# Eight residual stores issued from GpSimd's queue, and two PSUM banks shared in the odd mixer

## The chip, the cores and the metric

The kernel runs on one core of a Trainium2 chip. The metric is device microseconds (us) of one execution, the median of several runs. The engines are TensorE (PE in the rows; PEld is its weight load), VectorE (DVE), ScalarE (ACT), GpSimd (POOL) and SyncE (SP), which here only issues DMAs. Each engine works through its own instructions in order; an instruction that waits holds up all that stand behind it on its engine.

## The reference

One inference step of a two-layer trunk. The even layer (0) runs SSD heads and RG-LRU blocks, the odd layer (1) runs 4 GLA heads and 8 HGRN heads. Each layer is a mixer and a squared-ReLU MLP, each followed by a layer norm over the residual sum:

```python
for layer in range(DEPTH):
    if layer % 2 == 0:
        mixed, (a1, a2, a3, a4) = _even_mixer(h, segs, (ssd[j], ssd_conv[j], rg[j], rg_conv[j]), p, j)
        ...
    else:
        mixed, (a5, a6) = _odd_mixer(h, segs, (gla[j], hgrn[j]), p, j, layer)
        ...
    h = _layer_norm(ALPHA * h + mixed, p['ln1_g'][layer], p['ln1_b'][layer])
    h = _layer_norm(ALPHA * h + _sq_relu_mlp(h, p['mlp_w1'][layer], p['mlp_w2'][layer]),
                    p['ln2_g'][layer], p['ln2_b'][layer])
```

Both kinds of odd heads run the same gated linear attention, in chunks, over the prompt (16 meta and 512 prompt tokens) and over 8 samples of 8 tokens that start from given states:

```python
def step(s, inp):
    q_c, k_c, v_c, bl_c = inp
    o = jnp.einsum('bthk,bhkv->bthv', q_c, s)
    s = s * jnp.exp(bl_c)[..., None] + jnp.einsum('bshk,bshv->bhkv', k_c, v_c)
    return s, o
```

## The kernel before

Activations lie transposed in SBUF as 8 tiles of 128 features by T = 592 tokens (16 meta, 64 of the samples, 512 of the prompt), split into a high and a low float32r part (`h`). Every projection is a `Task`: two halves of the tokens, each 24 matmuls (L182) of 128x296 (some 128x280) into one of 5 PSUM banks (`pm`), after which ScalarE or VectorE reads the bank. Weights come as 512 KB units over SP's queue into 3 `raw` buffers (L120) and are split by ScalarE (L126) and VectorE (L127) a few units ahead.

Between the halves of tasks, `weave()` runs one step of each active generator, so that the small matmuls of the attention stand between the large ones on TensorE. These small products share the other 3 PSUM banks (`px`), which are handed out in turn; a fourth call of `px()` gets the first bank again, and its first matmul waits until that bank was read. Dependencies in PSUM are kept by whole banks. A scheduler then sets the final order on each engine, within what depends on what; the excerpts below show that order.

The places that the change touches:

- The end of layer 0's MLP (`after` in `mlp`). When the last half of the layer norm is done, GpSimd adds the norm's bias to each of the 8 residual tiles `rs[k]` (L645, 128x592), and each tile is stored to DRAM as `res` (L646, 296 KB), to be read back in layer 1's output projection (L511). SyncE issues the stores, between weight loads ahead of them and, behind them, the loads of the odd mixer: `wg2` (L1126, 64 KB, shown as `wg` in the rows), two masks, a head's states `sin` (L1159, 1 MB) and further weights.
- The start of the odd mixer. The tasks of the low-rank gate (L247, read into `lgf` by L1376) and of q, k and two v's of the first GLA head run half by half. Then `decays()` makes the decay `ls` of each of the 4 GLA heads from `wg2` and `lgf`: two matmuls (L1387, four rows in the trace), ScalarE (L1388) and VectorE (L1389, which writes `ls`). The tile `ls` of the second head lies where a residual tile lay, so its first writer waits for that tile's store; so do `q` of the first head and some others.
- `attend`, run for each head: nv = 2 value tiles for GLA, nv = 1 for HGRN. It transposes the prompt's values (L1195, two banks when nv = 2, copied to SBUF by L1196), the stacked sample values (L1218, one bank), and the samples' values (L1222, copied to `vs` by L1223); for nv = 2, L1222 has a bank of its own, of which it fills 256 of 512 columns. Later come transposes of the keys (L1243), scores (L1247, L1261, L1262), the samples' read of their states (L1270, 256 of 512 columns, copied by L1273), the samples' output (L1281, L1282: a bank of which 64 or 128 columns are used, copied by L1284) and the nine state products. For nv = 1 these are L1291 (four), L1295 (four) and L1298 (the ninth, a bank of its own); VectorE adds them into `sin` (`update`, L1287), and `sin` is stored (L1314). Then follow the prompt's states (L1321, VectorE L1322).

Of the kernel before, what the change touches and what calls it, by code (L numbers as in the profile page):

```python
# [14 lines left out]
P = 128  # L15
# [56 lines left out]
def _trunk(ctx, tc, nc, I, O):  # L72
    V, A, G, PE = nc.vector, nc.scalar, nc.gpsimd, nc.tensor
# [14 lines left out]
    def px():  # L88
        return pxp.tile([P, 512], F32, tag="px", name="px")
# [9 lines left out]
    def vc(name, i=0, n=1):  # L99
        o = VEC[name] + i  # L100
        return vec[:, o:o + n]

    def mk(name):
        a, b = MSK[name]
        return msk[:, a:b]

    ident, umask, lsmask, uxmask, lxmask, seqm, sel, blk = (
        mk(n) for n in ("ident", "u", "ls", "ux", "lx", "seq", "sel", "blk"))
# [205 lines left out]
    def new_h():  # L314
        return [act_tile(hp, "h") for _ in range(KT)]
# [231 lines left out]
    def mlp(H, layer, halves, last, keep=None):  # L547
# [3 lines left out]
        with ExitStack() as st:  # L551
# [3 lines left out]
            rs = [rp.tile([P, T], F32, tag="r", name="r") for _ in range(KT)]  # L555
# [83 lines left out]
            def after(i):  # L639
                if not last and out[0] is None:  # L640
                    out[0] = new_h()
                norm.finish(i, out[0])
                if keep is not None and i == 1:
                    for k in range(KT):
                        G.tensor_scalar(rs[k], rs[k], vc("ln2b", layer * 8 + k), None, OP.add)  # L645
                        nc.sync.dma_start(keep[:, k], rs[k])  # L646

            run([w1(0, f) for f in W1_ORDER[:4]], by_half=True)
            for k, f in enumerate(W1_ORDER[4:]):
# [3 lines left out]
            for b in range(4):  # L653
                if b < 3:
                    run([w1(b + 1, f) for f in W1_ORDER[:2]])
                    for j in range(0, KT, 2):
                        w2_pair(b, j)
                    run([w1(b + 1, f) for f in W1_ORDER[2:]])
                else:
                    run([w2(b, j) for j in range(KS)])  # L660
                    norm.shift()
                    run([w2(b, j) for j in range(KS, KT)], by_half=True, after=after)
# [458 lines left out]
    def odd_mixer(H, g):  # L1121
# [28 lines left out]
        def attend(q, k, ls, sc, qs, vf, gate, gcol, sdram, sout, pout, more):  # L1150
# [4 lines left out]
            nv = len(vf)  # L1155
            N = nv * P
# [33 lines left out]
            vs = sd.tile([P, 256], F32, tag="vs", name="vs")  # L1190
            for v in range(nv):
                p = px()
# [22 lines left out]
            p = px()  # L1215
            for v in range(nv):
                for j in range(2):
                    PE.transpose(p[0:120, j * N + v * P:j * N + (v + 1) * P],  # L1218
                                 vst[:, v, j].rearrange("p r c -> p (r c)").bitcast(F32), ident)
            u = px() if nv > 1 else p[:, 256:512]  # L1220
            for v in range(nv):
                PE.transpose(u[:, v * P:(v + 1) * P], vf[v][:, 16:144], ident)  # L1222
            A.copy(vs[:, 0:N], u[:, 0:N])  # L1223

            mw = sd.tile([P, 9, P], F32R, tag="mw", name="mw")
            mn = sd.tile([P, 2, 256], F32R, tag="mn", name="mn")
# [13 lines left out]
            p = px()  # L1240
# [5 lines left out]
            p = px()  # L1246
# [10 lines left out]
            p = px()  # L1257
# [6 lines left out]
                              cmask[:, None, 0:P].to_broadcast([P, 4, P]), p.rearrange("p (c n) -> p c n", n=P))  # L1264

            p = px()
            for j in range(2):
                for b in range(4):
                    w = 64 * b + 32 * j
                    PE.matmul(p[32 * b:32 * b + 32, 0:N], qm[:, w:w + 32], sin[:, 4 * j + b],  # L1270
                              start=(j == 0), stop=(j == 1), tile_position=(0, 32 * b))
# [7 lines left out]
            p = px()  # L1279
# [6 lines left out]
            def update(b, p, n):  # L1286
                V.tensor_tensor(sin[:, b:b + n], sin[:, b:b + n], p.rearrange("p (b n) -> p b n", b=n), OP.add)  # L1287

            if nv == 1:
                p = px()  # L1290
                PE.matmul(p, mn[0:120, 0, 0:P], mw[0:120, 0:4].rearrange("p b n -> p (b n)"), start=True, stop=True)  # L1291
                V.tensor_copy(S[:, 0, 0:P], p[:, 0:P])
                update(0, p[:, P:], 3)
                p = px()
                PE.matmul(p, mn[0:120, 1, 0:P], mw[0:120, 4:8].rearrange("p b n -> p (b n)"), start=True, stop=True)  # L1295
                update(3, p, 4)
                p = px()
                PE.matmul(p[:, 0:P], mn[0:120, 1, 0:P], mw[0:120, 8], start=True, stop=True)  # L1298
                update(7, p[:, 0:P], 1)
            else:  # L1300
                for b0 in range(0, 9, 2):
                    if b0 == 4:
                        yield
                    p = px()
                    n = min(2, 9 - b0)
                    for b in range(b0, b0 + n):
                        PE.matmul(p[:, (b - b0) * N:(b - b0 + 1) * N], mw[0:120, b], mn[0:120, 0 if b < 4 else 1],
                                  start=True, stop=True)
                    if b0 == 0:
                        V.tensor_copy(S[:, 0], p[:, 0:N])  # L1310
                        update(0, p[:, N:], 1)
                    else:
                        update(b0 - 1, p[:, 0:n * N], n)
# [3 lines left out]
            for c0 in range(0, 4, 4 // nv):  # L1317
                p = px()
# [7 lines left out]
            for v in range(nv):  # L1326
                p = px()
# [18 lines left out]
            rs = g("rs")  # L1346
            for c0, c1 in TAIL:
                p = px()[:, 0:c1 - c0]
# [46 lines left out]
        for h in range(4):  # L1395
            q, k, v0, v1 = (g(n) for n in ("q", "k", "v", "v"))
            tasks = [copy_task(q, TAIL), copy_task(k, FULL), copy_task(v0, FULL), copy_task(v1, FULL)]
            if h == 0:
                run([Task(H, FULL, lr_consume, small=wsr[:, 1])] + tasks[0:NB], by_half=True)
                run(tasks[NB:])  # L1400
            else:
                run(tasks)
            z = [g("zs"), g("zs")]
            while len(lsg) <= h:
                weave()
            active.append(attend(q, k, lsg[h], 1.0 / 16, P ** -0.5, (v0, v1), z, hg[:, 0:2],
                                 I["gst"][h], O["gla_s"][h], O["gla_p"][h], 1))
            run([silu_task(z[0]), silu_task(z[1])])
# [17 lines left out]
        for h in range(8):  # L1426
            if h == 0:
                run([f_task(0)])
            q, v, z = g("q"), g("v"), g("zs")
            run([silu_task(q), copy_task(v, FULL)])  # L1430
            ls, k = fk[h]
            active.append(attend(q, k, ls, 1.0, 0.5, (v,), (z,), hg[:, 2:3],
                                 I["hst"][h], O["hgrn_s"][h], O["hgrn_p"][h], 1 if h in (0, 7) else 0))
            run([silu_task(z)])
            if h < 7:
                run([f_task(h + 1)])
        return ys, st.close

    with ExitStack() as st:
        gp = pool("ge", NGE, stack=st)  # L1440

        def g(name="g"):
            return gp.tile([P, T], F32, tag="g", name=name)
# [174 lines left out]
```

## Time and profile before

| | |
|---|---|
| time before, median of 3 runs | 1945.5 us (1942.92 to 1948.19) |
| the profiled execution, its own time | 1947.84 us |
| its span in the trace | 1946.0 us |
| TensorE matmuls busy | 1869.0 us (96%) |
| VectorE / ScalarE / GpSimd busy | 1298.0 / 886.8 / 412.5 us |
| granted TensorE clock, mean | 0.98 |
| odd mixer's stretch of the span, about | 916 to 1460 us |

TensorE is busy nearly throughout, so that what matters are the stretches in which it is not. Times within the span count from its start. A clock of 1.00 is 2.4 GHz, 0.50 is 1.2 GHz.

### The profile page before, as it was taken

How to read it: one execution, taken by the hardware profiler on the slowest of the kernel's cores; microseconds unless marked ns; L12 is line 12 of the kernel's file. 1: busy time of each engine (PE TensorE's matmuls, PEld its weight loads, DVE VectorE, ACT ScalarE, POOL GpSimd, SP SyncE). 2: the span in 40 equal slices, each digit the busy share in tenths (PEclk: the TensorE clock that was granted, in tenths of full speed). 3: DMA queues.
4: the chain of work that ended last, by engine and by line, in shares of the span. 5: the costliest groups of instructions: out<-in, count | busy, mean ns of one | idle time of the engine just before them, and what ended most of it. 6: DMA issues, size and time to landing. Idle time of an engine off the chain costs nothing.

```text
span 1946.0 us, 33588 instructions
## 1 busy us (share of the span) xinstructions
PE 1869.0 (96%) x13854; PEld 1828.1 (94%) x13854; DVE 1298.0 (67%) x2035; ACT 886.8 (46%) x1550; POOL 412.5 (21%) x427
## 2 busy tenths in 40 slices
PE   8998899999999999999999999999999899999996
PEld 8998899898999999998899999999999899999996
DVE  7896767868875757458645456565665877676637
ACT  5333245623644444324544455665642563534333
POOL 3454423114000000135121222121203200000014
PEclk9999899999999999999999999999999899999998
DMA  6232221321223132312332223223232123141411
GB/s 203 90 118 72 68 100 55 121 88 55 77 66 109 66 109 66 114 61 93 109 111 102 99 96 106 89 86 104 90 114 66 66 66 123 52 130 44 130 55 49
DMA packets 69273, 175.97 MB, mean 90 GB/s; under 512 B 6624, under 2 KB 30304, under 8 KB 67968
## 3 DMA queue, kind: packets, MB, share of 16 engines
q1 hardware_dynamic: 69120, 173.82, 26.6%
q8 instruction: 109, 1.79, 0.4%
q14 instruction: 44, 0.36, 0.1%
HBM read 154.54 MB, written 19.25 MB: 89 GB/s over the span
## 4 chain that ended last, share of the span: by engine, by line
PE 76%; DVE 14%; ACT 4%; issue 3%; POOL 2%; DMA 0%; SPq 0%; ACTq 0%; DVEq 0%; POOLq 0%
PE pm L182 52%; PE pm L195 14%; DVE w L127 2%; DVE r L424 1%; PE px L1321 1%; POOL r L645 1%; PE px L1332 1%; PE px L1067 1%; PE px L1331 1%; POOL o L1356 1%; DVE h L496 1%; DVE r L494 1%; DVE k L1422 1%; DVE acc L708 1%; DVE r L478 1%
## 5 line engine op out<-in xcount | busy, mean ns | idle before, releaser
L182 PE MATMUL pm<-h,w 128*128 128x296 f32 (+2 forms) x8256 | 1184.3, 302 | 11.3 <-ACT h L308 5.5
L182 PEld LDWEIGHTS pm<-h,w 128*128 128x128 f32 x8256 | 1138.7, 190 | 23.3 <-issue 5.9
L127 DVE TENSOR_TENSOR w<-raw,w 128x1024 fp32r<-128x1024 f32 (+1 forms) x300 | 370.8, 1236 | 165.4 <-ACT w L126 164.7
L126 ACT CAST w<-raw 128x1024 fp32r<-128x1024 f32 (+1 forms) x300 | 304.0, 1014 | 300.8 <-PE pm L195 149.2
L195 PE MATMUL pm<-ff,w 128*128 128x296 f32 (+1 forms) x2016 | 273.3, 297 | 0.0
L195 PEld LDWEIGHTS pm<-ff,w 128*128 128x128 f32 x2016 | 271.9, 188 | 0.1
L620 POOL TENSOR_TENSOR sq<-sq 128x296 f32<-128x296 f32 (+1 forms) x32 | 21.5, 676 | 652.3 <-ACT sq L618 652.3
L182 PE MATMUL pm<-ff,w 128*128 128x296 f32 (+1 forms) x768 | 107.5, 302 | 0.0
L182 PE MATMUL pm<-m,w 128*128 128x296 f32 (+1 forms) x768 | 107.4, 302 | 0.0
L182 PEld LDWEIGHTS pm<-ff,w 128*128 128x128 f32 x768 | 106.1, 192 | 0.6 <-issue 0.3
L182 PEld LDWEIGHTS pm<-m,w 128*128 128x128 f32 x768 | 106.0, 192 | 0.6 <-issue 0.3
L607 DVE TENSOR_TENSOR ff<-sq,ff 128x888 fp32r<-128x888 f32 (+3 forms) x48 | 58.5, 1221 | 42.5 <-ACT ff L606 42.5
L588 ACT ACTIVATE sq<-pm 128x296 f32<-128x296 f32 (+1 forms) x96 | 37.8, 413 | 87.6 <-PE pm L182 66.3
L606 ACT CAST ff<-sq 128x888 fp32r<-128x888 f32 (+3 forms) x48 | 50.2, 1049 | 39.5 <-DVE sq L601 38.8
L1356 POOL TENSOR_TENSOR o<-o,zs 128x576 f32<-128x576 f32 x16 | 31.2, 1962 | 153.2 <-DVE o L1355 153.2
L1274 POOL TENSOR_TENSOR sin<-sin,ebl 128x1024 f32<-128x1024 f32 (+1 forms) x12 | 35.8, 2986 | 109.6 <-issue 104.6
L211 DVE TENSOR_TENSOR r<-r,pm 128x296 f32<-128x296 f32 (+1 forms) x96 | 43.6, 454 | 18.7 <-PE pm L195 18.1
L589 ACT ACTIVATE sq<-sq 128x296 f32<-128x296 f32 (+1 forms) x96 | 41.1, 449 | 0.8
L1361 ACT COPY v<-pm 128x296 f32<-128x296 f32 x32 | 12.9, 405 | 61.0 <-PE pm L182 61.0
L1322 DVE SCALAR_TENSOR_TENSOR S<-S,ebl,px 128x128 f32<-128x128 f32 (+1 forms) x48 | 18.7, 391 | 31.4 <-PE px L1321 31.2
L214 DVE TENSOR_TENSOR r<-r,pm 128x296 f32<-128x296 f32 (+1 forms) x72 | 32.6, 453 | 10.2 <-PE pm L195 10.2
L618 ACT ACTIVATE sq<-pm 128x296 f32<-128x296 f32 (+1 forms) x32 | 13.1, 415 | 56.8 <-PE pm L182 53.8
(389 smaller groups left out, 2270.6 us busy)
## 6 DMA issues: line engine op xcount, KB each, us to landing
raw<-in_w_dram SPq DMA_DIRECT2D x252, 512.0 KB, 3.3
sin<-in_sst_dram SPq DMA_DIRECT2D x8, 512.0 KB, 3.8
out_ssd_s_dram<-sin SPq DMA_DIRECT2D x8, 512.0 KB, 3.2
sin<-in_gst_dram SPq DMA_DIRECT2D x4, 1024.0 KB, 5.8
out_gla_s_dram<-sin SPq DMA_DIRECT2D x4, 1024.0 KB, 3.9
sin<-in_hst_dram SPq DMA_DIRECT2D x8, 512.0 KB, 4.4
out_hgrn_s_dram<-sin SPq DMA_DIRECT2D x8, 512.0 KB, 3.5
xt<-in_x_dram SPq DMA_DIRECT2D x16, 148.0 KB, 4.1
```

Source lines behind the costliest of these rows:

```text
L126: A.copy(w[:, 0, :n], r)
L127: V.tensor_tensor(w[:, 1, :n], r, w[:, 0, :n].bitcast(F32), OP.subtract)
L182: PE.matmul(p[:, :n], w[:, a, ks], xs[k][:, b, c0:c1], start=(k == 0 and i == 0), stop=(k == KT - 1 and i == 2))
L195: PE.matmul(p[:, :n], w[:, a, ks], xs[k][:, b, :n], start=(first and k == 0 and i == 0), stop=(k == 3 and i == 2), skip_group_check=True)
L211: V.tensor_tensor(y, y, p[:, :n], OP.add)
L214: V.tensor_tensor(y, y, p[:, :n], OP.subtract)
L588: A.activation(q, p, AF.Relu)
L589: A.activation(q, q, AF.Square)
L606: A.copy(t[:, 0, a:e, :n], s[:, a + 1:e + 1, :n])
L607: V.tensor_tensor(t[:, 1, a:e, :n], s[:, a + 1:e + 1, :n], t[:, 0, a:e, :n].bitcast(F32), OP.subtract)
L1274: G.tensor_tensor(sin, sin, ebl[:, 0:8].unsqueeze(2).to_broadcast([P, 8, N]), OP.mult)
L1356: G.tensor_tensor(o[v][:, c], o[v][:, c], gate[v][:, c], OP.mult)
```

## The change

Three edits. The residual stores are issued by GpSimd (`G.dma_start`) in place of SyncE. In a GLA head (nv = 2) the transposes of the samples' values no longer take a bank of their own; they are written later, into the free half of the bank that holds the read of the samples' states. In an HGRN head (nv = 1) the ninth state product goes into free columns of the bank that holds the samples' output, and its `update` is written ahead of the other two.

```diff
@@ mlp, after()
                     for k in range(KT):
                         G.tensor_scalar(rs[k], rs[k], vc("ln2b", layer * 8 + k), None, OP.add)
-                        nc.sync.dma_start(keep[:, k], rs[k])
+                        G.dma_start(keep[:, k], rs[k])
@@ attend()
-            u = px() if nv > 1 else p[:, 256:512]
-            for v in range(nv):
-                PE.transpose(u[:, v * P:(v + 1) * P], vf[v][:, 16:144], ident)
-            A.copy(vs[:, 0:N], u[:, 0:N])
+
+            def samples(u):
+                for v in range(nv):
+                    PE.transpose(u[:, v * P:(v + 1) * P], vf[v][:, 16:144], ident)
+                A.copy(vs[:, 0:N], u)
+
+            if nv == 1:
+                samples(p[:, 256:384])
...
             p = px()
+            if nv == 2:
+                samples(p[:, 256:512])
             for j in range(2):
                 for b in range(4):
                     w = 64 * b + 32 * j
...
             if nv == 1:
+                PE.matmul(p[:, P:2 * P], mn[0:120, 1, 0:P], mw[0:120, 8], start=True, stop=True)
+                update(7, p[:, P:2 * P], 1)
                 p = px()
...
-                p = px()
-                PE.matmul(p[:, 0:P], mn[0:120, 1, 0:P], mw[0:120, 8], start=True, stop=True)
-                update(7, p[:, 0:P], 1)
```

The numbers of instructions of each kind stay the same. After the change lines behind L646 have other numbers: L1387 is L1392, L1389 is L1394, L1222 is L1223, L1261 and L1262 are L1265 and L1266, L1270 is L1276, L1281 is L1287, L1291 and L1295 are L1299 and L1303, L1298 (the ninth product) is L1296, and L1321 is L1326. In the excerpts of the order, what an instruction waits for stands in brackets: an engine's name means an earlier instruction of that engine, DMAHW a transfer that SyncE issued, DMASW one that GpSimd issued (DMASW0 the first of the eight stores, DMASW7 the last).

On SyncE the eight stores are gone from between the weight loads and `wg2`. On GpSimd the eight additions used to stand together but for two memsets; now two additions and two stores take turns, four times, and the four memsets stand behind them.

TensorE at the start of the odd mixer, behind the low-rank gate's second half; first before:

```order
L247 MATMUL pm<-h,wsr 32x296 [waits DVE_49]
L182 MATMUL pm<-h,w 128x296 [waits Activation_49]
L182 MATMUL pm<-h,w 128x296 x23
L1387 MATMUL px<-lgf,wg_9320 128x296 [waits DMAHW7_49]
L1387 MATMUL px<-lgf,wg_9320 128x296 [waits Activation_49]
L182 MATMUL pm<-h,w 128x296 x24
L1387 MATMUL px<-lgf,wg_9320 128x296
L1387 MATMUL px<-lgf,wg_9320 128x296 [waits DVE_49]
L182 MATMUL pm<-h,w 128x296 x24
```

(of the two task halves, q and k, ahead of the first L1387 one stands here), and now:

```order
L247 MATMUL pm<-h,wsr 32x296 [waits DVE_49]
L1392 MATMUL px<-lgf,wg_9320 128x296 [waits DMAHW7_49]
L182 MATMUL pm<-h,w 128x296 [waits Activation_49]
L182 MATMUL pm<-h,w 128x296 x23
L1392 MATMUL px<-lgf,wg_9320 128x296
...
L1392 MATMUL px<-lgf,wg_9320 128x296
L1392 MATMUL px<-lgf,wg_9320 128x296 [waits DVE_49]
L182 MATMUL pm<-h,w 128x296 [waits Activation_49]
L182 MATMUL pm<-h,w 128x296 x23
L1392 MATMUL px<-lgf,wg_9320 128x296 [waits DVE_49] x2
```

The first product with `wg2` moved ahead of the q half, its second ahead of the k half. The left-out rows are the halves of k and of the first v.

VectorE at the same place, now (the L1394 are those of the first head and of the second):

```order
L127 TENSOR_TENSOR w<-raw,w 128x1024 [waits DMAHW4_49,Activation_49]
L1394 TENSOR_SCALAR ls<-px,vec 128x296 [waits Activation_49] x2
L1148 TENSOR_TENSOR vst<-v,vst 128x2x40 [waits Activation_49] x2
L127 TENSOR_TENSOR w<-raw,w 128x1024 [waits DMAHW5_49,Activation_49]
L1397 TENSOR_TENSOR ls<-ls,lt 128x592 [waits DVE_49,Activation_49]
L1166 SCALAR_TENSOR_TENSOR ls<-rmask,ls 128x592 [waits DMAHW0_49,DVE_49]
L1178 TENSOR_TENSOR kx<-ls 128x4x64 [waits DVE_49]
L127 TENSOR_TENSOR w<-raw,w 128x1024 [waits DMAHW6_49,PE_49,Activation_49]
L1394 TENSOR_SCALAR ls<-px,vec 128x296 [waits DMASW7_49,Activation_49,Pool_49]
L1394 TENSOR_SCALAR ls<-px,vec 128x296 [waits Activation_49]
```

The second head's L1394 waited for the last store before too, as a DMAHW; the store is now issued behind the others in GpSimd's order.

ScalarE's copy of the first head's q half (L1361, now L1366) waits for the first store, now DMASW0, and moved behind the copy of the gate's second half (L1376, now L1381).

TensorE in the second GLA head, before:

```order
L1218 MATMUL px<-msk,vst 120x128 [waits DVE_49]
L1218 MATMUL px<-msk,vst 120x128
L1222 MATMUL px<-msk,v 128x128 [waits Activation_49]
L1222 MATMUL px<-msk,v 128x128
L182 MATMUL pm<-h,w 128x296 x24
L1243 MATMUL px<-msk,e_10234 128x128 [waits DVE_49,Activation_49]
L1243 MATMUL px<-msk,e_10234 128x128 x3
```

and now, some 60 matmuls later, behind the scores:

```order
L1265 MATMUL px<-e_10232,kx 128x64
L1266 MATMUL px<-e_10232,kx 128x64
L1223 MATMUL px<-msk,v 128x128 [waits Activation_49]
L1223 MATMUL px<-msk,v 128x128
L182 MATMUL pm<-h,w 128x296 x4
L1276 MATMUL px<-sin,qm_9331 32x256 [waits DMAHW4_49,Activation_49]
L1276 MATMUL px<-sin,qm_9331 32x256 x7
L182 MATMUL pm<-h,w 128x296 x20
```

The two transposes moved behind the scores, and the read of the states behind four large matmuls and a wait for ScalarE, which is the copy of the transposes' half of the bank. The other GLA heads read alike.

TensorE in the second HGRN head, before:

```order
L1291 MATMUL px<-mw,mn 128x512 [waits DVE_49]
L1295 MATMUL px<-mw,mn 128x512 [waits PE_49]
L182 MATMUL pm<-h,w 128x296 x8
L1298 MATMUL px<-mw,mn 128x128 [waits DVE_49,PE_49]
L182 MATMUL pm<-h,w 128x296 x16
L1321 MATMUL px<-vt,kt 128x128 [waits Activation_49]
```

and now:

```order
L1299 MATMUL px<-mw,mn 128x512 [waits DVE_49]
L1303 MATMUL px<-mw,mn 128x512 [waits PE_49]
L182 MATMUL pm<-h,w 128x296 x10
L1296 MATMUL px<-mw,mn 128x128 [waits Activation_49]
L182 MATMUL pm<-h,w 128x296 x14
L1326 MATMUL px<-vt,kt 128x128 [waits DVE_49,PE_49]
```

The ninth product stands at nearly the same place, but waits for ScalarE (the copy of the samples' output out of the bank) in place of VectorE, and the first product of the prompt's states now waits for VectorE.

## Rows read from the trace of the kernel before

**Rows 1.** The page's head and the chain that ended last, by engine.

```profile
span 1946.0 us, 33588 instructions
...
PE 76%; DVE 14%; ACT 4%; issue 3%; POOL 2%; DMA 0%; SPq 0%; ACTq 0%; DVEq 0%; POOLq 0%
```

**Rows 2.** Waits of PE, 925 to 1460 us: us in total, times, longest.

```profile
PE px L1298 <- DVE sin L1287: 5.4, 6, 0.9
PE px L1222 <- ACT vt L1196: 4.4, 3, 1.5
PE px L1387 <- DMA wg<-in_wg_dram: 3.6, 1, 3.6
PE px L1243 <- DVE e L1203: 1.9, 1, 1.9
PE px L1249 <- DVE kst L1148: 0.5, 1, 0.5
```

**Rows 3.** PE's timeline, 928 to 941 us: start, us, instruction, [idle before <-releaser].

```profile
928.68 2.24 PE L1387 MATMUL px<-lgf,wg 32*128 32x296 f32 x4 [3.56 <-DMA wg<-in_wg_dram]
930.85 5.67 PE L182 MATMUL pm<-h,w 128*128 128x296 f32 x24
936.44 1.26 PE L1387 MATMUL px<-lgf,wg 32*128 32x296 f32 x4
937.63 3.52 PE L182 MATMUL pm<-h,w 128*128 128x296 f32 x24
```

**Rows 4.** Windows: us, busy of PE, PEld, DVE, ACT, POOL, then PEclk, DMA share, GB/s.

```profile
933.00:935.00 2.00, 2.00 (x10) 2.00 (x10) 1.97 (x2) 0.00 (x0) 0.00 (x0) 0.50 0.96 379
```

**Rows 5.** The chain that ended last, 905 to 940 us: start, us, what.

```profile
909.99 4.31 POOL r L645 x2
...
914.47 7.43 POOL r L645 x4
...
922.67 3.50 POOL r L645 x2
```

**Rows 6.** The additions and the stores by line: duration in ns min/median/max, first and last start.

```profile
L645 POOL TENSOR_SCALAR r<-r,vec x8: 1761/1766/2340, 910.0 to 924.4; 128x592 f32<-128x592 f32 x8
...
L646 SPq DMA_DIRECT2D res<-r x8: 319/320/327, 912.4 to 926.2; - x8
...
DMA to landing us min/median/max: 2.1/2.1/2.5
```

**Rows 7.** ACT's and DVE's timeline, 914 to 942 us.

```profile
915.88 0.38 ACT L1361 COPY q<-pm 128x280 f32<-128x280 f32 x1
...
918.54 0.40 ACT L1376 COPY lgf<-pm 32x296 f32<-32x296 f32 x1 [1.40 <-PE pm L247]
...
939.08 0.95 DVE L1389 TENSOR_SCALAR ls<-px,vec 128x296 f32<-128x296 f32 x2
```

**Rows 8.** All engines' timeline in the second GLA head, 1004 to 1013 us.

```profile
1007.52 1.06 ACT L1196 COPY vt<-px 128x512 f32<-128x512 f32 x2
...
1008.14 0.44 PE L1222 MATMUL px<-msk,v 128*128 128x128 f32 x2 [1.47 <-ACT vt L1196]
...
1008.91 0.23 DVE L1148 TENSOR_TENSOR kst<-e,kst 128x80 fp32r<-128x80 f32 x1
...
1010.40 0.41 ACT L1223 COPY vs<-px 128x256 f32<-128x256 f32 x1
...
1012.29 0.39 PE L1249 MATMUL px<-msk,kst 128*120 128x128 f32 x2
```

**Rows 9.** All engines' timeline in the second HGRN head, 1204 to 1212 us.

```profile
1205.62 0.21 ACT L1284 COPY o<-px 128x64 f32<-128x64 f32 x1
...
1207.41 1.14 DVE L1287 TENSOR_TENSOR sin<-sin,px 128x384 f32<-128x384 f32 x2
...
1208.09 0.30 PE L1298 MATMUL px<-mw,mn 120*128 120x128 f32 x1 [0.90 <-DVE sin L1287]
...
1210.88 0.35 DVE L1322 SCALAR_TENSOR_TENSOR S<-S,ebl,px 128x128 f32<-128x128 f32 x1 [1.78 <-PE px L1321]
```

## The prediction

> **What bounds the kernel now.** I read the page first. The chain that ended last runs through TensorE for 76% of the span of 1946.0 us [rows 1], and TensorE's instructions are not changed in number or size. So the change is worth what it takes from TensorE's waits and from stretches at a low clock. The list of TensorE's waits in the odd mixer holds five [rows 2], 15.8 us in all, and three of them are what the edits touch: L1298 for VectorE (six times, 5.4 us), L1222 for ScalarE (three times, 4.4 us), L1387 for the load of `wg2` (once, 3.6 us). No other of TensorE's waits in this stretch is longer than 1.9 us, so behind a removed one there is nearly always matmul work at hand. VectorE and ScalarE are far from full. The timelines around each of the three waits then show what is late, and what would be late next.
>
> **Edit 1, the stores; what goes.** In the chain, GpSimd's additions (4.31 + 7.43 + 3.50 = 15.2 us for eight) lead from 909.99 us to 926.17 us [rows 5], and SyncE, which stands at each store until its tile is added, can issue the load of `wg2` only then. TensorE waits 3.56 us for it [rows 3]. What follows is slow too: the four rows of L1387 take 2.24 us against 1.26 us the next time, and 24 large matmuls 5.67 against 3.52 us [rows 3], with a granted clock of 0.50 (1.2 GHz) [rows 4]. The loss is 3.56 + 0.98 + 2.15 = 6.7 us. With the stores gone from SyncE, `wg2` is issued behind a weight load that was already out before 904 us, and is there long before TensorE asks for it at about 918.4 us. I take the 6.7 us as removed; below it only a wait behind SyncE's own loads could keep some of it, and nothing in its queue there waits.
>
> **Edit 1, what it adds.** Two waits on GpSimd's stores, priced by an unknown, c, the time that issuing one store takes on GpSimd; no row shows it. SyncE's issue takes 0.32 us [rows 6], which is the lower bound. As the upper bound I take an addition over the same tile, 1.77 us [rows 6], as if GpSimd passed over it once more. These are far apart and neither is near in kind: I take their middle, c = 1.05 us.
>
> First, ScalarE's copy of q waits for store 0, which is issued after two additions, at 909.99 + 4.31 = 914.3 us [rows 5]. A store lands 2.1 us after SyncE begins its issue, so 1.8 us after its end [rows 6]; here 914.3 + 1.05 + 1.8 = 917.2 us. The copy now stands behind the gate's second copy, which starts at 918.54 us [rows 7] since it waits for TensorE, so the store is covered, by 1.6 us. But TensorE's q half needs the bank of this copy: one product with `wg2` (0.6 us, below) ends at 918.9 us, the two copies (0.40 and 0.38 us, one behind the other [rows 7]) at 919.3 us. A new wait of 0.4 us.
>
> Second, VectorE's L1394 of the second GLA head waits for store 7. GpSimd is done with all additions after 15.2 us and with the stores 8c later, so store 7 lands at 909.99 + 15.2 + 8c + 1.8 = 927.0 + 8c: 935.4 us at c = 1.05. Who waits for that L1394 is TensorE: the `px` banks turn in threes, and the second product of the third head's decay needs the bank that this L1394 (0.5 us [rows 7]) reads. TensorE comes there after the halves of q, k and two v's, 3.5 us each [rows 3], and between them four single products with `wg2` (of which two make 1.19 us, from 936.44 to 937.63 us [rows 3]): 919.3 + 4 x 3.5 + 4 x 0.6 is 935.7 us. So the bank is free at 935.9 us and TensorE waits 0.2 us. At c = 0.32 the store lands at 929.6 us and nothing waits; at c = 1.77 it lands at 941.2 us, TensorE waits 6.0 us and, as after the 3.56 us, would run slow for another 3.1 us. Behind the waiting L1394 stand weight splits (L127) for units that TensorE reaches later still. The four memsets and the first head's `e4` on GpSimd end at about 937 us as before; their readers come some 10 us later. Edit 1 is 6.7 - 0.4 - 0.2 = 6.1 us; its bounds are 6.3 and 6.7 - 0.4 - 6.0 - 3.1 = -2.8 us.
>
> The Trainium skill, "DMA: Bandwidth & Descriptors", section "Latency and other measured facts", states about 1 us to the first byte for a GpSimd DMA against about 0.6 us for one from SyncE. If that difference were all, c would be near 0.7 us as an estimate, store 7 would be covered and edit 1 worth 6.3 us; no run here shows it yet.
>
> **Edit 2, the values' transposes (GLA).** In three of four heads L1222 waits 1.47 us, because it takes the bank that ScalarE's second-to-last copy (L1196, started at 1007.52 us behind its exponentials) has not yet read [rows 8]. The new place asks for a bank whose copy is long done, so 4.4 us go. Does the wait move to the next instruction? `kst` is ready at 1009.14 us and L1249 starts at 1012.29 us [rows 8]; 1.47 us earlier it still has 1.7 us of room, and the key transposes before it need the first L1196, done at about 1008.1 us (half of the 1.06 us), some 2 us before they come. New is L1276 behind the copy `vs`: 0.41 us [rows 8] and its start, against four matmuls of 3.52 / 24 = 0.147 us [rows 3], 0.59 us. I take 0.1 us in each of four heads, at most the whole copy, 1.6 us in all. Edit 2 is 4.0 us, from 2.8 to 4.4.
>
> **Edit 3, the ninth product (HGRN).** In six of eight heads it waits 0.90 us until VectorE has read the bank of the first four (L1287, 1207.41 us, behind VectorE's work on the next head) [rows 9]. Now it waits for the copy L1284, which ends at 1205.83 us, two us earlier, with ten matmuls ahead of it: 5.4 us go. L1326 takes over the wait for L1287; it comes 0.9 us sooner, at about 1209.5 us, and both updates have ended at 1208.55 us [rows 9]. VectorE sat idle 1.78 us ahead of L1322 [rows 9], so it has room. Edit 3 is 5.4 us; the lower bound, if another wait takes each over, is nothing.
>
> The Trainium skill's "PSUM — Partial Sum Buffer", section "PSUM bank collisions raise a hardware error", says that reads and writes of one bank by two engines must be kept apart by bank, not by address. That speaks against sharing banks: each half-used bank now makes TensorE wait for a copy of the other half. These are the waits for ScalarE just priced; the sums hold them already.
>
> **Sum.** 6.1 + 4.0 + 5.4 = 15.5 us. The profiled execution took 1947.84 us, 1.84 us more than its span, and would take 1932.3 us; it stood 2.3 us above the median of 1945.5 us, from which the same sum gives 1930.0 us. I forecast 1931 us, between the two and nearer to the median. Everything at its better bound is 6.3 + 4.4 + 5.4 = 16.1 us (1929 us), at its worse -2.8 + 2.8 + 0, nothing; these do not come together often.
>
> **Rivals.**
>
> 1. GpSimd's issue is slow (c between 1.4 and 2.5 us): VectorE stands at L1394 for store 7, TensorE behind it, the clock falls again. At c = 1.77 edit 1 costs 2.8 us and the whole gives -2.8 + 4.0 + 5.4 = 6.6 us: 1939 us. For it speaks that GpSimd's additions stretch from 1.77 to 2.34 us while VectorE works beside them [rows 6], so issuing may stretch as well; against it that VectorE has less work there after 916 us. The Trainium skill's "SBUF — State Buffer", section "SBUF: two separate sides", states a cause of such a stretch, VectorE holding the port through which GpSimd writes descriptors; VectorE's operations there are of other kinds than it names, and no run here shows it. Chance 0.12.
>
> 2. The other side: slower, by the same mechanism. The 6.3 + 4.0 + 5.4 = 15.7 us of gains are eaten when TensorE waits 12.6 us at that bank and then runs slow for 3.1 us, store 7 landing at 935.7 + 12.6 - 0.5 = 947.8 us, c = 2.6 us; slower by over 0.3% needs c = 3.3 us, a time of about 1951 us. No row of GpSimd's small instructions is near that. Chance 0.05.
>
> 3. The released waits come back at the next instruction, because what is late is the other engine's chain and not the bank: edits 2 and 3 give little and edit 1 stands, 1945.5 - 6.1 = 1939.4 us. The wait of L1249 for `kst` and of L1243 for VectorE [rows 2] show that TensorE catches up with VectorE in two heads already; the slack worked out above speaks against it. Chance 0.08.
>
> 4. Nothing measurable, because a store lands late for q (ScalarE and all behind it stand) and parts of 2 and 3 go as well. Chance 0.03.
>
> **How the numbers follow.** The forecast case (12 to 17 us gained, 1928 to 1934 us) has 0.72. The runs before spread over 5 us, so 0.3% (5.8 us) is about what tells a change from none. The range goes from 1927 us (all at its better bound, less half of that spread) to 1940 us, which takes in rivals 1 and 3 for the most part. Faster by over 0.3% is below 1939.7 us: the forecast, half of rivals 1 and 3, and a little: 0.83. Slower: 0.05 and a rest, 0.06. Same: 0.11.
>
> **What would show it.** After the change: no wait of L1392 for `wg2` and a clock of 1.00 from 918 to 940 us; no wait at L1223; none of 0.9 us at the ninth product (L1296); TensorE's waits in the odd mixer near 4 us in place of 15.8. The duration of L646 on GpSimd gives c; the last store's landing against VectorE's second pair of L1394 shows whether the new wait is there. I am wrong if TensorE waits several us between 934 and 950 us for VectorE, if ScalarE's q copy waits for store 0, or if L1276, L1247 or L1326 each wait where L1222 and L1298 did.

## The result

The changed kernel took 1926.0 us (median of 4 runs, 1924.49 to 1926.09) against 1946.4 us for the kernel before (4 runs, 1942.92 to 1948.19): a ratio of 0.990, 95% interval 0.988 to 0.991, so 20.4 us less, in an interval of about 17 to 24. Forecast were 15.5 us less (1931, range 1927 to 1940). The direction was right; the gain was 5 us larger, and the median lies 1 us below the range. Measured twice more beside the experiments, the same kernel took 1929.3 and 1929.6 us, 16.5 and 16.3 us less than before.

The page of the changed kernel, its head and the chain that ended last [rows 1]:

```profile
span 1924.3 us, 33593 instructions
...
PE 80%; DVE 13%; ACT 3%; issue 3%; POOL 0%; DMA 0%; SPq 0%; ACTq 0%; DVEq 0%; POOLq 0%
```

GpSimd's 2% in the chain were the additions ahead of the stores; they are off it. TensorE's waits, 890 to 1420 us (us in total, times, longest), against [rows 2]:

```profile
PE px L1247 <- DVE e L1203: 1.9, 1, 1.9
PE pm L247 <- DVE h L496: 1.7, 2, 1.3
PE pm L247 <- ACT h L495: 0.7, 1, 0.7
PE pm L247 <- ACT lgf L1381: 0.5, 1, 0.5
PE px L1253 <- DVE kst L1148: 0.5, 1, 0.5
```

The three waits that the edits touch are gone, and no wait of this list has come up in their place; the first and the last row are those of L1243 and L1249 before. What the list leaves out as too short is a wait that the prediction had priced: in the four GLA heads the weight load of L1276 stands for ScalarE's copy of the samples' values, 0.7 us in all. The cause of the longest one stands in SyncE's timeline, first before, then after: the load of `wg2` was issued behind the eight stores and now leaves 25 us sooner.

```profile
912.35 14.15 SPq L646 DMA_DIRECT2D res<-r  x8
926.60 0.38 SPq L1126 DMA_DIRECT2D wg<-in_wg_dram  x1
```

```profile
901.47 0.42 SPq L1126 DMA_DIRECT2D wg<-in_wg_dram  x1
```

In the timeline of TensorE there is no stall at the products with `wg2` (now L1392) [rows 3]:

```profile
913.23 2.35 PE L247 MATMUL pm<-h,wsr 128*32 128x296 f32 x16 [0.54 <-ACT lgf L1381]
915.51 0.76 PE L1392 MATMUL px<-lgf,wg 32*128 32x296 f32 x2
916.20 3.52 PE L182 MATMUL pm<-h,w 128*128 128x296 f32 x24
...
920.34 6.79 PE L182 MATMUL pm<-h,w 128*128 128x296 f32 x48
927.06 1.26 PE L1392 MATMUL px<-lgf,wg 32*128 32x296 f32 x4
928.25 3.51 PE L182 MATMUL pm<-h,w 128*128 128x296 f32 x24
931.70 1.26 PE L1392 MATMUL px<-lgf,wg 32*128 32x296 f32 x4
...
936.19 1.26 PE L1392 MATMUL px<-lgf,wg 32*128 32x296 f32 x4
```

Each 24 large matmuls take 3.5 us, and the window has a granted clock of 1.00 where 0.50 stood [rows 4] (us, then busy of PE, PEld, DVE, ACT, POOL, PEclk, DMA share, GB/s):

```profile
918.00:940.00 22.00, 22.00 (x142) 19.36 (x141) 15.77 (x22) 17.55 (x31) 13.07 (x15) 1.00 0.53 180
```

The stores on GpSimd by line [rows 6], and then, from the timeline, its first additions and last stores [rows 5] and VectorE's wait for the last store:

```profile
L646 POOL DMA_DIRECT2D res<-r x8: 539/570/778, 911.6 to 926.4; - x8
...
  DVE ls L1394: 1.5, 1
...
DMA to landing us min/median/max: 2.4/3.3/6.5
```

```profile
907.20 4.50 POOL L645 TENSOR_SCALAR r<-r,vec 128x592 f32<-128x592 f32 x2 [2.17 <-DVE h L496]
...
925.82 1.13 POOL L646 DMA_DIRECT2D res<-r  x2
...
931.41 0.96 DVE L1394 TENSOR_SCALAR ls<-px,vec 128x296 f32<-128x296 f32 x2 [1.45 <-DMA res<-r]
```

So the unknown c is 0.57 us, a landing takes 2.4 to 6.5 us after the issue began, and VectorE stands 1.45 us for the last store without TensorE noticing. The second GLA and the second HGRN head on TensorE [rows 8, 9]:

```profile
996.77 0.60 PE L1218 MATMUL px<-msk,vst 128*120 128x128 f32 x4
997.12 3.51 PE L182 MATMUL pm<-h,w 128*128 128x296 f32 x24
1000.47 0.60 PE L1247 MATMUL px<-msk,e 128*128 128x128 f32 x4
...
1006.14 0.39 PE L1223 MATMUL px<-msk,v 128*128 128x128 f32 x2
1006.29 0.78 PE L182 MATMUL pm<-h,w 128*128 128x296 f32 x4
...
1191.50 0.39 PE L1303 MATMUL px<-mw,mn 120*128 120x512 f32 x1
1191.73 1.52 PE L182 MATMUL pm<-h,w 128*128 128x296 f32 x10
1193.10 0.22 PE L1296 MATMUL px<-mw,mn 120*128 120x128 f32 x1
1193.16 2.13 PE L182 MATMUL pm<-h,w 128*128 128x296 f32 x14
1195.13 0.38 PE L1326 MATMUL px<-vt,kt 128*128 128x128 f32 x2
```

What these stretches cost is read from start to start, against the same instructions of the kernel before (PE's timeline, rows that were not shown yet):

```profile
916.21 2.30 PE L247 MATMUL pm<-h,wsr 128*32 128x296 f32 x16
918.35 6.77 PE L182 MATMUL pm<-h,w 128*128 128x296 f32 x48
...
945.58 1.26 PE L1387 MATMUL px<-lgf,wg 32*128 32x296 f32 x4
...
1006.08 0.60 PE L1218 MATMUL px<-msk,vst 128*120 128x128 f32 x4
...
1011.69 0.60 PE L1243 MATMUL px<-msk,e 128*128 128x128 f32 x4
...
1205.71 0.39 PE L1295 MATMUL px<-mw,mn 120*128 120x512 f32 x1
1205.94 1.25 PE L182 MATMUL pm<-h,w 128*128 128x296 f32 x8
...
1208.23 2.39 PE L182 MATMUL pm<-h,w 128*128 128x296 f32 x16
1210.46 0.38 PE L1321 MATMUL px<-vt,kt 128*128 128x128 f32 x2
```

| stretch, us | before | after | less |
|---|---|---|---|
| edit 1: L247's second half to the fourth head's product with `wg2` | 29.37 | 22.96 | 6.41 |
| edit 2: L1218 to the keys' transposes, per head | 5.61 | 3.70 | 1.91 |
| edit 3: L1295 (L1303) to L1321 (L1326), per head | 4.75 | 3.63 | 1.12 |

Of the 1.91 us of a GLA head about 0.27 come back where the transposes stand now, since the difference between the starts of the same large matmul shrinks by that much there: 0.15 us for the transposes themselves (1006.14 to 1006.29 us) and the rest a wait for ScalarE's copy. That leaves 1.64 us a head. The three edits together are 6.4 + 3 x 1.6 + 6 x 1.12 = 18 us. The profiled spans differ by 21.7 us, and 3.0 of them were there before TensorE came to the first instruction that an edit moves: L247 starts at 913.23 and not 916.21 us.

### The profile page after: what moved, and what is told of

Same layout as the page of the kernel before. It is cut to its first block, busy times and chain, and to the rows that moved or that the text cites. A ratio compares the mean times of both kernels' runs of the same rounds, so it can differ in the third digit from the quotient of the medians.

```text
span 1924.3 us, 33593 instructions
## 1 busy us (share of the span) xinstructions
PE 1858.2 (97%) x13854; PEld 1819.0 (95%) x13854; DVE 1297.1 (67%) x2035; ACT 886.0 (46%) x1550; POOL 417.2 (22%) x435
## 4 chain that ended last, share of the span: by engine, by line
PE 80%; DVE 13%; ACT 3%; issue 3%; POOL 0%; DMA 0%; SPq 0%; ACTq 0%; DVEq 0%; POOLq 0%
PE pm L182 55%; PE pm L195 14%; DVE w L127 1%; DVE r L424 1%; DVE h L496 1%; DVE r L494 1%; PE px L1326 1%; DVE r L478 1%; PE px L1337 1%; PE px L1336 1%; PE px L1067 1%; DVE lnq L447 1%; DVE acc L708 1%; PE px L925 1%; DVE ln L447 1%
## 5 line engine op out<-in xcount | busy, mean ns | idle before, releaser
L1361 POOL TENSOR_TENSOR o<-o,zs 128x576 f32<-128x576 f32 x16 | 31.3, 1967 | 148.7 <-DVE o L1360 148.7
L1366 ACT COPY v<-pm 128x296 f32<-128x296 f32 x32 | 12.9, 405 | 58.6 <-PE pm L182 58.6
L495 ACT ACTIVATE h<-r,vec 128x296 fp32r<-128x296 f32 (+1 forms) x48 | 23.8, 536 | 31.5 <-DVE r L494 31.5
```

## The experiments

**Theory 1**: the gain is the sum of three independent edits, each worth what it costs from start to start; the remaining 2 us are stretches at a low clock that fall elsewhere in unchanged code by chance. **Theory 2**, the rival: what exceeds the forecast is caused by the change, in the code ahead of the stores or because fewer stalls keep the clock up elsewhere.

**One edit at a time, from the kernel before.** Each takes its hunks of the diff shown ahead of the prediction.

```diff
-                        nc.sync.dma_start(keep[:, k], rs[k])
+                        G.dma_start(keep[:, k], rs[k])
```

> Edit 1 alone: the eight residual stores go out on GpSimd's own queue, nothing else changes. Theory 1 (the gain is three separate edits, each at what it costs from start to start on TensorE, and the remaining 2 us are low-clock stretches that fall elsewhere by chance): 6.4 us off, a ratio of 0.9967, some 1940 where before is 1946.4; no TensorE wait at the gate's low-rank product, wg2 landed by 905, the second GLA head's wait for its samples and the ninth product's wait still there. Theory 2 (the gain outside the odd mixer is caused by the change: the code ahead of the stores and the clock run better with the stores elsewhere): 8.5 us or more, 0.9956 or less, and the gate's second half again 2 to 3 us early.

Edit 2 alone (`samples(p[:, 256:512])` in the new place):

> Edit 2 alone: in the three later GLA heads the transposes of the samples' values come behind the fold products and share a bank with the two products after them. Theory 1: 4.8 us off (1.6 a head from start to start), ratio 0.9975, some 1941.6; the idle rows of the wait alone, as the prediction had it, would give 4.0, 0.9979. Theory 2 (part of the whole gain belongs to no single edit, because fewer stalls keep the clock up elsewhere): 4.0 or less. The 3.56 us wait for wg2 stays.

Edit 3 alone (the ninth product into `p[:, P:2 * P]`):

> Edit 3 alone: the ninth state product of the HGRN heads goes ahead of the eight others into the second half of the bank of the product before it. Theory 1: 6.3 to 7.2 us off (1.05 to 1.2 a head, six heads), ratio 0.9963 to 0.9968, some 1939 to 1940; the idle rows alone would give 5.4, 0.9972. Theory 2: 5.4 or less. The wait for wg2 and the three waits for the samples stay.

Both of them:

> Edits 2 and 3 together, the stores still on SyncE's queue. Theory 1: the sum of the two alone, 11 to 12 us, ratio 0.9938 to 0.9943, some 1935; what is left to the whole change is edit 1. Theory 2 (the edits help each other through the clock): more than the two alone added, 13 us or more, 0.9933 or less.

| kernel | us, median | before | less | ratio, 95% | L247's second half starts |
|---|---|---|---|---|---|
| edit 1 | 1937.6 | 1945.6 | 8.0 | 0.9961 (0.9947 to 0.9975) | 913.55 |
| edit 2 | 1941.6 | 1945.6 | 4.0 | 0.9979 (0.9971 to 0.9987) | 916.81 |
| edit 3 | 1938.5 | 1945.6 | 7.1 | 0.9963 (0.9950 to 0.9977) | 912.41 |
| edits 2 and 3 | 1933.2 | 1945.6 | 12.4 | 0.9939 (0.9925 to 0.9953) | 912.41 |

By the times alone the theories can't be told apart. Edit 1's 8.0 us lie between the 6.4 and the 8.5 expected, edit 2's 4.0 are what theory 2 had, edits 2 and 3 together lie between 12 and 13, and the intervals are 3 to 5 us wide. The single edits add up to 19.1 us, edits 2 and 3 to 11.1 where together they gave 12.4; that shows no surplus of the whole.

The traces decide. Every kernel has these four places on TensorE: L247's second half, the fourth head's product with `wg2`, L1218 of the first HGRN head, and the first product of the prompt's states in the seventh HGRN head (L1321 before, L1326 in the changed kernel), the last head with a wait. Before, they start at 916.21, 945.58, 1160.28 and 1390.33 us, in the changed kernel at 913.23, 936.19, 1146.04 and 1369.38. The stretches between them, us:

| trace | edit 1's stretch | GLA heads | HGRN heads | together | less |
|---|---|---|---|---|---|
| before | 29.37 | 214.70 | 230.05 | 474.12 | |
| edit 1 | 22.96 | 214.60 | 230.06 | 467.62 | 6.50 |
| edit 2 | 29.52 | 209.80 | 230.08 | 469.40 | 4.72 |
| edit 3 | 29.39 | 214.62 | 223.33 | 467.34 | 6.78 |
| edits 2 and 3 | 29.39 | 209.83 | 223.36 | 462.58 | 11.54 |
| the changed kernel | 22.96 | 209.85 | 223.34 | 456.15 | 17.97 |

Each edit shortens its own stretch and leaves the two others as they were, within 0.15 us; the three single edits add up to 18.0 us and the whole is 18.0 us. So theory 2 falls in its second form. Its first form, the code ahead of the stores, falls by the column of the start of L247: nothing that edits 2 and 3 change has run at that point, yet their traces stand 3.8 us ahead of the kernel before there, and that of edit 2 0.6 us behind.

**Only `wg2` moved.** Is the queue ahead of `wg2` all of edit 1?

```diff
-        nc.sync.dma_start(wg2, I["wg2"])
+        nc.scalar.dma_start(wg2, I["wg2"])
```

> The kernel before, but the 64 KB of wg2 are asked for by ScalarE's queue and no longer by SyncE's behind the eight stores; the stores stay where they were. Theory 1 (edit 1 is worth what the wait for wg2 costs TensorE, with the slow clock behind it, and the queue ahead of wg2 is its only cause): as much as the stores on GpSimd, 5.7 to 6.4 us, 1939 to 1940; no wait for wg2, and no stretch at a granted clock of 0.50 between 915 and 945 us. A rival (moving the stores itself brings the gain: less traffic beside the weights, or VectorE and GpSimd otherwise timed): 2 us or less, 1943 or above, with a new wait for rmask or the stores in its place.

It took 1940.0 us against 1945.8 (0.9970, 0.9959 to 0.9981): 5.8 us less, with the stores where they had been. The load was issued at 912.3 us, and the granted clock was 1.00 from 915 to 945 us. TensorE's timeline of this kernel:

```profile
913.21 2.34 PE L247 MATMUL pm<-h,wsr 128*32 128x296 f32 x16 [0.55 <-ACT lgf L1376]
...
936.16 1.26 PE L1387 MATMUL px<-lgf,wg 32*128 32x296 f32 x4
```

22.95 us, as with the stores on GpSimd (22.96). The load's place in SyncE's queue is the whole of edit 1's gain in this stretch; the stores' own place is worth nothing there. VectorE now stands 0.35 us for rmask, still behind the stores, and TensorE doesn't notice. With rmask moved as well, and edits 2 and 3:

> Edits 2 and 3, and instead of edit 1 the loads of wg2 and rmask on ScalarE's queue, with the stores left on SyncE's. Theory 1: the same three waits are gone, so the time of the changed kernel, 1925 to 1928. The rival that the stores' place matters by itself: near edits 2 and 3 alone, 1931 to 1934.

1926.8 us (0.9910, 0.9897 to 0.9923), beside the changed kernel on the same chip:

> The changed kernel once more, on the chip of the other three. Theory 1: 18 us from the three edits and 2 from where low-clock stretches fall, so 1926 to 1928, ratio 0.989 to 0.991, against 19.1 us for the three edits run alone and added up. Theory 2 (they help each other): more than 21 us.

1929.3 us (0.9916, 0.9903 to 0.9929), 16.5 us less and so under what theory 1 expected, and once more on another chip:

> The changed kernel on the chip of the other two. If its start-to-start gain is 18 us and the rest is where low-clock stretches fall, 16 to 20 us below the kernel before.

1929.6 us (0.9917, 0.9903 to 0.9931). The variant and the changed kernel can't be told apart by time, nor by the four places: 456.17 us from L247 to the seventh HGRN head, against 456.15, 456.09 and 456.10 in the three traces of the changed kernel. These three start L247's second half at 913.23, 914.39 and 916.76 us and have spans of 1924.3, 1926.7 and 1929.7 us. The spread of 5.4 us thus lies in code that no edit touches, 3.5 of it ahead of L247 and 1.9 behind the seventh HGRN head. Stretches of a granted clock of 0.50 fall at different places there: ahead of 890 us the first has six of them, 30.6 us together, the third eight, 40.8 us.

**How near rival 1 was.** Every store sent twice:

```diff
                         G.dma_start(keep[:, k], rs[k])
+                        G.dma_start(keep2[:, k], rs[k])
```

> The changed kernel with every residual store issued twice by GpSimd, the second time into a tile that nobody reads: the issue time per column tile doubles to some 1.1 us, which is the value that the prediction had taken for one store. If GpSimd's issue time is as near the path as the prediction had it (rival 1: it decides between 1.05 and 3.3 us a tile), the last store lands 4 to 5 us later than at 931.4 and VectorE, held at the third head's decay, lets TensorE wait for 1 to 4 us: 1927 to 1930. If there is slack enough, VectorE alone waits and the time stays at 1926 within 1 us.

1933.0 us, 3.7 above the changed kernel on the same chip; from L247 to the seventh HGRN head it is 459.8 us, 3.7 more too. In TensorE's timeline the wait of rival 1 is there (L1393 and L1395 are L1392 and L1394 of the changed kernel), and the 24 large matmuls behind it take 4.96 us where they took 3.52 (the row has 23 of them, since the view's window ends at 947 us):

```profile
941.61 0.83 PE L1393 MATMUL px<-lgf,wg 32*128 32x296 f32 x2 [1.61 <-DVE ls L1395]
942.38 4.83 PE L182 MATMUL pm<-h,w 128*128 128x296 f32 x23
```

To tell GpSimd's time from the doubled traffic, GpSimd was to be held with memsets:

```diff
                         G.dma_start(keep[:, k], rs[k])
+                        for _ in range(7):
+                            G.memset(idle, 0.0)
```

> The changed kernel, each store sent once, but GpSimd is kept busy behind each by seven small memsets of a tile that nobody reads, some 0.55 us together by the 0.09 us or so that the smallest memsets take. That is the time that the second set of stores took from GpSimd, without its traffic. If it was GpSimd's time that cost the 3.7 us of that run, the last store lands at 935 to 937 us again, VectorE waits some 3 us and TensorE 1 to 2, and the time is 3 to 4 us above the changed kernel on the same chip. If it was the doubled traffic and the later landings, VectorE's wait is under 3 us, TensorE's wait gone, and the time within 1 us of the changed kernel.

It told nothing: the scheduler put the memsets, on which nothing depends, at the start of the program (1.2 to 12.0 us), and the kernel ran as the changed one, 1926.2 us. Then with the delay inside the chain:

```diff
+                        G.tensor_scalar(rs[k][:, 0:180], rs[k][:, 0:180], 0.0, None, OP.add)
                         G.dma_start(keep[:, k], rs[k])
```

> The changed kernel with GpSimd held inside the chain, since the memsets of the run before were not placed behind the stores: between a tile's addition and its store, zero is added to its first 180 columns, some 0.54 us by the 1.77 us of an addition over 592. Eight times that is 4.3 us, as long as the second set of stores held GpSimd, without its traffic. If the time at which the last store leaves is what matters, it lands at 935 to 936 in place of 931.4 us on the clock of the changed kernel's trace, TensorE, which had 0.4 us of room there, waits 3 to 4 us and runs slow behind it, and the time is 1931 to 1934. If it was the doubled traffic that cost the time when every store was sent twice, TensorE waits for less than 1 us there and the time stays within 1 us of the changed kernel's 1926 to 1930.

1926.7 us (0.9905, 0.9889 to 0.9922). By time and wait this is what was expected if the doubled traffic had cost the time, but it can't be read so. The delay was 0.66 us a tile, and the last store landed 5.6 us later than in the changed kernel, counted from the first addition: 938.23 - 908.37 = 29.9 against 931.41 - 907.20 = 24.2 us. But the scheduler's new order has the third head's decay, and not the second's, stand for that store, as in the kernel with double stores; TensorE needs it a head later (its timeline, VectorE and TensorE):

```profile
938.23 0.96 DVE L1395 TENSOR_SCALAR ls<-px,vec 128x296 f32<-128x296 f32 x2 [1.39 <-DMA res<-r]
...
938.81 0.76 PE L1393 MATMUL px<-lgf,wg 32*128 32x296 f32 x2 [0.29 <-DVE ls L1395]
```

These two kernels share this order, so they can be compared: with double stores the last began 25.4 us after the first addition and released VectorE after 31.1 us; here it began after 24.3 and released it after 29.9. TensorE's wait grew from 0.29 to 1.61 us, 1.3 us for a release that came 1.2 us later. Most of that, 1.0 us, is that the last store left later. The double traffic itself adds 0.2 us.

The stores behind all additions:

```diff
                     for k in range(KT):
                         G.tensor_scalar(rs[k], rs[k], vc("ln2b", layer * 8 + k), None, OP.add)
-                        G.dma_start(keep[:, k], rs[k])
+                    for k in range(KT):
+                        G.dma_start(keep[:, k], rs[k])
```

> The changed kernel, but GpSimd adds all eight tiles first and then sends the eight stores one behind the other. The eight additions end some 4 us sooner and all stores then leave within 4.6 us, so the last is sent at about the same time and lands no sooner, if anything later as eight share the DMA engines. ScalarE's copy of q waits for the first store, which now leaves at about 922 in place of 912 us. If a late first store was the danger that the prediction saw there, TensorE waits several us behind that copy and the time is 3 us or more above the changed kernel; if not, within 1 us.

1932.0 us, 2.4 above the changed kernel measured beside it; single runs of the two overlap, but from L247 to the seventh HGRN head this trace is 5.5 us longer (461.6 us). The scheduler sent two stores after three additions, one after six and five at the end, so the first left at 913.8 and not 922 us. ScalarE's copy of q waited 2.5 us for it, and TensorE didn't wait for that. But the last store landed 3.1 us later, on a clock that runs as that of the first trace up to there (L247 at 913.21 us), and in the timeline of TensorE and VectorE rival 1 stands in full:

```profile
931.66 0.76 PE L1393 MATMUL px<-lgf,wg 32*128 32x296 f32 x2
...
934.55 0.96 DVE L1395 TENSOR_SCALAR ls<-px,vec 128x296 f32<-128x296 f32 x2 [4.63 <-DMA res<-r]
...
935.13 1.35 PE L1393 MATMUL px<-lgf,wg 32*128 32x296 f32 x2 [2.70 <-DVE ls L1395]
936.41 5.29 PE L182 MATMUL pm<-h,w 128*128 128x280 f32 x24
```

The window behind it, columns as above, with a granted clock of 0.52:

```profile
935.00:941.00 6.00, 5.87 (x22) 5.09 (x23) 5.72 (x9) 3.19 (x4) 0.00 (x0) 0.52 0.18 48
```

L1195 of the first head starts at 946.17 instead of 940.74 us: 5.4 us lost by a store that is released 3.14 us later. Of those 3.14 us 2.70 reached TensorE, so the changed kernel has 0.4 us of room at this place, and no more.

## Why the prediction was right in direction and too small

**What the edits remove** was read rightly: the three waits are gone, no other has taken their place, and each single edit gives a gain of its own.

**The step that failed is the price of a wait.** The prediction said that the change "is worth what it takes from TensorE's waits" and set 0.90 and 1.47 us for one, the idle rows, with 5.4 and 4.4 us for all and 16.1 us as the better bound of the whole. From start to start one wait costs more. In the HGRN head the eight matmuls ahead of the wait have a row of 1.25 us, but in the flow eight of them start within 8 x 2.23 / 16 = 1.11 us (the sixteen from 1208.23 to 1210.46 us): rows of matmuls overlap, and the idle time is counted from the end of the last one, 0.14 us after the next could have started. The ninth product then holds TensorE 0.14 us until the next start (1208.09 to 1208.23), and in the changed kernel 0.06 (1193.10 to 1193.16). 0.90 + 0.14 + 0.08 = 1.12 us, the measured difference. In the GLA head the next instruction can start 0.35 us after L1218 does (996.77 to 997.12), while L1218's row is 0.60 long: 1.47 + 0.25 + 0.20 for the transposes = 1.92 us, of which 0.27 come back. The wait that takes its place was priced nearly rightly, 0.1 us a head against 0.12. So edit 2 was 4.8 to 4.9 and not 4.0 us, edit 3 6.7 and not 5.4. What had been called the better bound was none.

**Edit 1** came out at 6.4 us against 6.1. From one head's product to the next it is 7.76 us where the clock was low (928.68 to 936.44 [rows 3]) and 4.64 in the changed kernel (927.06 to 931.70): 3.1 us, as counted. The stall is 3.6 us from start to start too: from the first of 48 large matmuls to the product behind them it was 10.33 us (918.35 to 928.68) and is 6.72 (920.34 to 927.06). Of these 6.7 us 0.2 come back since the first head's two products are now apart, 2 x 0.69 us (915.51 to 916.20) in place of 1.19 (927.06 to 928.25), and 0.1 since L247's half takes 2.28 us until the next instruction starts, in place of 2.14. Of the two waits priced as added, 0.4 for the copy of q and 0.2 for the last store, neither appeared. The first did not even where the first store began 2.1 us later (stores last, 913.80 against 911.65 us); in the two kernels with the other order TensorE waited 0.2 us for that copy. A wait of 0.54 us for ScalarE's first copy of `lgf` is new in the first trace. It belongs to the clock ahead of it and not to the edit: the 14 traces have it, with 0.5 us or more, where the 87 large matmuls ahead of L247 took 12.2 us (the kernel with only `wg2` moved among them), with 0.16 at 12.45 us, and not at 12.5 us or more (both repeats of the changed kernel among them).

**Rival 1's place was right, its two sizes wrong, and by luck they cancelled.** The prediction had the last store land 17.0 + 8c = 25.4 us after the first addition; measured were 24.2. c was 0.57 and not 1.05 us, which takes off 3.8 us; issuing hardly stretched, 0.78 us at most, for the first store. But a landing on this queue is not the 2.1 us of SyncE's stores [rows 6]: the last store's issue begins at 926.39 us and VectorE goes on at 931.41, 5.0 us later. With the prediction's margin of -0.2 us and the 0.4 us measured, its chance of 0.12 was not too high. The Trainium skill, "DMA: Bandwidth & Descriptors", section "Latency and other measured facts", puts the first byte of a GpSimd DMA some 0.4 us later than that of one from SyncE; the medians to landing here differ by 1.2 us (3.3 against 2.1), and the last store's landing by 2.9. Rival 3 did not come up: behind the removed waits L1253's 0.5 us and L1247's 1.9 us are what they were.

**The rest.** With the three measured prices the sum is 18 us, the forecast would have been about 1928.5, and the lower edge, worked out as 1927 with the bound of 16.1 us, would have been 1925; the 1926.0 us would have lain within. The mis-sized price is half of the 5 us. The other half is luck: 18 us lie in the intervals of all three measurements of the changed kernel (20.4 us, 17 to 24; 16.5, 14 to 19; 16.3, 13 to 19), one of which came out above and two below. What sets them apart is not an edit, since the stretch that the edits touch is the same within 0.1 us in the three traces; why the low-clock stretches fall where they do remains open.

## What to carry to other kernels

Price a wait of TensorE from the start of a matmul ahead of it to the start of one behind it, and take off what the same instructions need where nothing waits; the idle row is the lower bound, here by 0.2 to 0.25 us a wait, with nine such waits 2 us. Before a store is moved to another queue, ask which small load stood behind it: moving only that load gave the same gain in that stretch, and VectorE did not come to stand for the last store. And count how far each new wait is from deciding: here 0.4 us of room lay ahead of a loss of 5 us.

## What the chip showed that was not expected

A 296 KB store is issued by GpSimd in 0.54 to 0.78 us (SyncE 0.32) and lands 2.4 to 6.5 us after its issue began, where SyncE's took 2.1 to 2.5; whether the queue itself or the weights and states that move at the same time make it slow was not separated. A wait of 2.7 us was followed by 24 matmuls in 5.29 us at a granted clock of 0.52 over the window, as the 3.56 us before by 24 in 5.67 us [rows 3, 4]; behind the wait of 1.61 us they took 4.96, behind that of 0.29 us 3.52. Two executions of one program can differ by 5 us without any change to it: the three traces of the changed kernel do, and the stretch of 456 us that the edits touch is the same in them within 0.1 us.
